# Grouped softmax on one core: tiles of 24 groups in four buffers, in place of 16 groups in six

## The chip, the core and the metric

The kernel runs on one core of a Trainium2 chip. A core has a matrix engine (PE), VectorE (DVE in the profile), ScalarE (ACT), GpSimd (POOL) and SyncE (SP), which run their own instruction streams and meet at semaphores. Data moves between the chip's main memory (DRAM here, HBM in the profile) and the on-chip memory of 128 partitions (SBUF) by 16 DMA engines, which all queues share. The metric is the device time of one execution in microseconds; the median of four runs is compared.

## The reference

The input is 4 x 4096 rows of 4352 floats. Each row falls into 8 groups of 544, and each group gets its own softmax:

```python
def reference(x):
    B, N, D = x.shape          # 4, 4096, 4352
    G = 8
    Dg = D // G                # 544
    x_g = x.reshape(B, N, G, Dg)
    x_g = x_g - x_g.max(axis=-1, keepdims=True)
    exp = np.exp(x_g)
    out = exp / exp.sum(axis=-1, keepdims=True)
    return out.reshape(B, N, D).astype(np.float32)
```

285.2 MB are read and 285.2 MB written. A group is 544 x 4 = 2176 bytes, and there are 131,072 groups, 1024 for each of the 128 partitions.

## The kernel before

The 16,384 rows are cut into 64 tiles of 256 rows. A tile puts two consecutive rows on each partition, 16 groups or 34,816 bytes that lie side by side in DRAM (L33, L34). Six buffers `xt` of that size take the tiles in turn (tile t in buffer t mod 6, L51); exp, sums and products are done in place.

For each tile the work goes round the engines:

- SP issues the load (L126) after the store of the tile six before from the same buffer has landed (L123). The last tile is loaded in two halves (L129).
- ScalarE takes exp of the whole tile in one instruction (L75), as soon as the load has landed.
- VectorE sums the groups into `sums`, which lies in PSUM (L85), takes reciprocals of the 16 sums into `rs` (L87), and multiplies the tile by them, each broadcast over its group (L90).
- POOL waits for that product and issues the store (L138). The stores of the last two tiles are issued by SP instead (L134).

So loads go through SP's queue (q1 in the profile) and stores through POOL's (q0), and within each queue the order is that of the tiles. The instruction streams of all engines are written out tile by tile, with no loop.

No maximum is subtracted on this way. Instead all sums are kept in PSUM until the end, and `judge` (L97 to L119) tests whether one lies outside 1e-6 to 1e30: the largest and the smallest of the sums by two reductions each (L101, L103), two comparisons (L106, L109), a product with ones on PE that counts over the partitions (L113), a sum and a cast (L117, L119). Only where the count isn't zero is everything computed again, with the maximum subtracted (from L156). With this input that branch isn't taken.

Of the kernel before, what the change touches and what calls it, by code (L numbers as in the profile page):

```python
# [9 lines left out]
def kernel(  # L10
# [6 lines left out]
    G = 8  # L17
    P = 128
    R = 2
    NT = 6  # L20
    RG = R * G
# [4 lines left out]
    nt = N // (P * R)  # L26
    LAST = 2
    LOW, HIGH = 1e-6, 1e30
    f32 = mybir.dt.float32
    X = mybir.AxisListType.X  # L30
    Exp = mybir.ActivationFunctionType.Exp
    op = mybir.AluOpType
    xt = xf.rearrange("(t p r) d -> t p (r d)", p=P, r=R)  # L33
    ot = of.rearrange("(t p r) d -> t p (r d)", p=P, r=R)  # L34

    landed = [tc.alloc_semaphore(f"landed{b}") for b in range(NT)]
    stored = [tc.alloc_semaphore(f"stored{b}") for b in range(NT)]
    last_landed = tc.alloc_semaphore("last_landed")
# [4 lines left out]
    scaled = tc.alloc_semaphore("scaled")  # L43
    tested = tc.alloc_semaphore("tested")
# [6 lines left out]
    bufs = [ctx.enter_context(nc.sbuf_tensor(f"xt{b}", [P, R * D], f32)) for b in range(NT)]  # L51
    rs = ctx.enter_context(nc.sbuf_tensor("rs", [P, NT, RG], f32))
    mx = ctx.enter_context(nc.sbuf_tensor("mx", [P, RG], f32))
    sm = ctx.enter_context(nc.sbuf_tensor("sm", [P, RG], f32))
    one = ctx.enter_context(nc.sbuf_tensor("one", [P, 1], f32))
    extreme = ctx.enter_context(nc.sbuf_tensor("extreme", [P, 4], f32))
    outside = ctx.enter_context(nc.sbuf_tensor("outside", [P, 4], f32))
    count = ctx.enter_context(nc.sbuf_tensor("count", [1, 1], f32))
    verdict = ctx.enter_context(nc.sbuf_tensor("verdict", [1, 1], mybir.dt.int32))
    half = nt // 2  # L60
    sums = [ctx.enter_context(nc.psum_tensor(f"sums{h}", [P, half, RG], f32)) for h in range(2)]
    found = ctx.enter_context(nc.psum_tensor("found", [1, 4], f32))

    parts = [(t, slice(0, RG)) for t in range(nt - 1)]
    parts += [(nt - 1, slice(r * G, (r + 1) * G)) for r in range(R)]

    def grouped(b):
        return bufs[b][:, :].rearrange("p (g d) -> p g d", d=Dg)

    def groups(t, g):  # L70
        return grouped(t % NT)[:, g, :]

    def scalar_exp(n):
        t, g = parts[n]
        i = nc.scalar.activation(out=groups(t, g), in_=groups(t, g), func=Exp, scale=1.0)  # L75
        if g.start == 0:
            i.wait_op(landed[t % NT], 16 * (t // NT + 1), "sem-ge")
        else:
            i.wait_op(last_landed, 16, "sem-ge")
        i.then_inc(exp_done, 1)  # L80

    def vector_scale(n):
        t, g = parts[n]
        s = sums[t // half][:, t % half, g]
        nc.vector.reduce_sum(out=s, in_=groups(t, g), axis=X).wait_op(  # L85
            exp_done, n + 1, "sem-ge").then_inc(sum_done, 1)
        nc.vector.reciprocal(out=rs[:, t % NT, g], in_=s).wait_op(  # L87
            sum_done, n + 1, "sem-ge").then_inc(rec_done, 1)
        xg = groups(t, g)
        nc.vector.tensor_tensor(  # L90
            out=xg,
            in0=xg,
            in1=rs[:, t % NT, g].unsqueeze(2).to_broadcast([P, g.stop - g.start, Dg]),
            op=op.mult,
        ).wait_op(rec_done, n + 1, "sem-ge").then_inc(scaled, 1)

    def judge():  # L97
        nc.vector.memset(one[:, :], 1.0).then_inc(tested, 1)  # L98
        flat = [s[:, :, :].rearrange("p t g -> p (t g)") for s in sums]
        for h in range(2):  # L100
            nc.vector.tensor_reduce(  # L101
                out=extreme[:, h:h + 1], in_=flat[h], axis=X, op=op.max).then_inc(tested, 1)
            nc.vector.tensor_reduce(  # L103
                out=extreme[:, 2 + h:3 + h], in_=flat[h], axis=X, op=op.min).then_inc(tested, 1)
        nc.vector.wait_ge(tested, 5)
        nc.vector.tensor_scalar(  # L106
            out=outside[:, 0:2], in0=extreme[:, 0:2], scalar1=HIGH, scalar2=None,
            op0=op.is_gt).then_inc(tested, 1)
        nc.vector.tensor_scalar(  # L109
            out=outside[:, 2:4], in0=extreme[:, 2:4], scalar1=LOW, scalar2=None,  # L110
            op0=op.is_lt).then_inc(tested, 1)
        nc.tensor.wait_ge(tested, 7)
        nc.tensor.matmul(  # L113
            out=found[:, :], lhsT=one[:, :], rhs=outside[:, :],
            start=True, stop=True).then_inc(counted, 1)
        nc.vector.wait_ge(counted, 1)
        nc.vector.reduce_sum(out=count[:, :], in_=found[:, :], axis=X).then_inc(tested, 1)  # L117
        nc.vector.wait_ge(tested, 8)
        nc.vector.tensor_copy(out=verdict[:, :], in_=count[:, :]).then_inc(judged, 1)  # L119

    for t in range(nt):
        if t >= NT:
            nc.sync.wait_ge(stored[t % NT], 16 * (t // NT))  # L123
        tile_in = bufs[t % NT]
        if t < nt - 1:
            nc.sync.dma_start(out=tile_in[:, :], in_=xt[t]).then_inc(landed[t % NT], 16)  # L126
        else:
            for r in range(R):
                nc.sync.dma_start(  # L129
                    out=tile_in[:, r * D:(r + 1) * D], in_=xt[t, :, r * D:(r + 1) * D],  # L130
                ).then_inc(landed[t % NT] if r < R - 1 else last_landed, 16)
# [13 lines left out]
    for n in range(len(parts)):  # L145
        scalar_exp(n)
# [74 lines left out]
```

## Time and profile before

| What | Value |
|---|---|
| median of four runs | 1325.15 us (1325.03 to 1325.25) |
| the profiled execution, its own time | 1325.08 us |
| its span in the trace | 1323.3 us |
| VectorE busy | 1199.3 us, 91% |
| ScalarE busy | 478.7 us, 36% |
| POOL busy | 33.3 us, 3% |
| read and written | 285.21 MB each, 431 GB/s over the span |
| load, median from issue to landing | 41.4 us |
| POOL's store, median from issue to landing | 55.4 us |
| ScalarE's wait for loads, in total | 815.3 us |
| SP's wait (L126) for stores, in total | 1196.1 us |

The span is the time from the first to the last instruction of the program in the trace; the run's own time has a little more around it. In the rows that follow, a timeline line is start, duration, engine, line of the kernel, operation, what it writes and reads, and in brackets how long the engine had been idle and what ended that. A group line has the number of instructions, then their busy time in all and the mean of one in ns, then the idle time before them. A window line has from:to and length, busy time of PE, PEld, DVE, ACT and POOL (with the number of instructions), PE's clock, the share of the DMA engines that was busy, and GB/s. A DMA queue's row has packets, MB, and the share of the 16 engines' time that its packets took.

### The profile page before, as it was taken

The numbers are of one execution on the slowest core, as the hardware profiler recorded it, in microseconds if no ns is written. First come the engines' busy times: TensorE is split into PE (matmuls) and PEld (weight loads), VectorE is DVE, ScalarE is ACT, GpSimd is POOL, SyncE is SP. The second block draws the span as 40 slices with busy tenths as digits, with TensorE's granted clock in tenths as the row PEclk, the third lists the DMA queues.
The fourth block names the chain that finished last, engine by engine and source line by source line (L and its number), as shares of the span: only waits on it lengthen the run. The fifth ranks groups of instructions, "written<-read, shape, count | busy, mean of one in ns | idle before, by whom it ended". The sixth has DMA issues, their size and how long they took to land.

```text
span 1323.3 us, 475 instructions
## 1 busy us (share of the span) xinstructions
PE 0.2 (0%) x2; PEld 0.1 (0%) x2; DVE 1199.3 (91%) x204; ACT 478.7 (36%) x66; POOL 33.3 (3%) x66
## 2 busy tenths in 40 slices
PE   0000000000000000000000000000000000000000
PEld 0000000000000000000000000000000000000000
DVE  3999999999898988989989889898898988989895
ACT  4443342433424324234243342433424334243231
POOL 0000000000000000000000000000000000000000
DMA  9999999999999999999999999999999999999999
GB/s 404 421 437 429 430 438 435 430 431 437 434 429 435 436 434 429 436 436 433 428 437 437 430 430 437 434 431 433 436 434 430 435 436 433 429 436 437 430 429 389
DMA packets 18581, 570.47 MB, mean 431 GB/s; under 512 B 2064, under 2 KB 2064, under 8 KB 2064
## 3 DMA queue, kind: packets, MB, share of 16 engines
q1 hardware_dynamic: 9648, 294.13, 51.6%
q0 software_dynamic: 8928, 276.30, 48.3%
q14 instruction: 5, 0.04, 0.0%
HBM read 285.21 MB, written 285.21 MB: 431 GB/s over the span
## 4 chain that ended last, share of the span: by engine, by line
another core or an unknown queue 67%; DVE 21%; DMA 8%; ACT 1%; SPq 1%; issue 0%; PE 0%; POOLq 0%
DVE xt L90 10%; DVE sums L85 10%; DMA xt<-in_x_dram 4%; DMA out_dram<-xt 4%; ACT xt L75 1%; SPq L126 1%; DVE rs L87 0%; DVE extreme L103 0%; DVE extreme L101 0%; PE found L113 0%; DVE outside L106 0%; DVE count L117 0%; DVE verdict L119 0%; DVE outside L109 0%
## 5 line engine op out<-in xcount | busy, mean ns | idle before, releaser
L75 ACT ACTIVATE xt<-xt 128x8704 f32<-128x8704 f32 (+1 forms) x65 | 477.4, 7345 | 815.3 <-DMA xt<-in_x_dram 815.3
L85 DVE TENSOR_REDUCE sums<-xt 128x16 f32<-128x8704 f32 (+1 forms) x65 | 590.6, 9086 | 104.7 <-ACT xt L75 104.7
L90 DVE TENSOR_TENSOR xt<-xt,rs 128x8704 f32<-128x8704 f32 (+1 forms) x65 | 590.5, 9085 | 2.3
L138 POOL DMA_DIRECT2D out_dram<-xt x62 | 33.1, 533 | 1233.2 <-DVE xt L90 1233.2
L87 DVE RECIPROCAL rs<-sums 128x16 f32<-128x16 f32 (+1 forms) x65 | 16.6, 256 | 2.2
L144 ACT ACT_TABLE_LOAD x1 | 1.3, 1283 | 0.9 <-PEq L205 0.9
L101 DVE TENSOR_REDUCE extreme<-sums 128x1 f32<-128x512 f32 x2 | 1.4, 684 | 0.0
L103 DVE TENSOR_REDUCE extreme<-sums 128x1 f32<-128x512 f32 x2 | 1.4, 682 | 0.0
L117 DVE TENSOR_REDUCE count<-found 1x1 f32<-1x4 f32 x1 | 0.1, 149 | 0.3 <-PE found L113 0.3
L113 PE MATMUL found<-outside,one 128*1 128x4 f32 x2 | 0.2, 166 | 1308.3 <-DVE outside L109 1308.3
L106 DVE TENSOR_SCALAR outside<-extreme 128x2 f32<-128x2 f32 x1 | 0.2, 170 | 0.0
L119 DVE CAST verdict<-count 1x1 int32<-1x1 f32 x1 | 0.1, 141 | 0.0
L113 PEld LDWEIGHTS found<-outside,one 128*1 128x1 f32 x2 | 0.1, 80 | 1308.3 <-DVE outside L109 1308.3
L109 DVE TENSOR_SCALAR outside<-extreme 128x2 f32<-128x2 f32 x1 | 0.2, 163 | 0.0
L205 POOL MEMSET const-float32-0.0<- 128x1 f32 x1 | 0.1, 99 | 0.3 <-issue 0.3
L205 POOL MEMSET const-bfloat16-1.0<- 128x1 bf16 x1 | 0.1, 102 | 0.0
L205 POOL MEMSET const-float32-1.0<- 128x1 f32 x1 | 0.1, 99 | 0.0
L205 POOL MEMSET const-uint8-127<- 128x1 uint8 x1 | 0.1, 99 | 0.0
L98 DVE MEMSET one<- 128x1 f32 x1 | 0.1, 59 | 0.0
## 6 DMA issues: line engine op xcount, KB each, us to landing
xt<-in_x_dram SPq DMA_DIRECT2D x63, 4352.0 KB, 41.4
out_dram<-xt POOLq DMA_DIRECT2D x62, 4352.0 KB, 55.4
out_dram<-xt SPq DMA_DIRECT2D x2, 4352.0 KB, 20.6
xt<-in_x_dram SPq DMA_DIRECT2D x2, 2176.0 KB, 43.3
```

Source lines behind the costliest of these rows:

```text
L75: i = nc.scalar.activation(out=groups(t, g), in_=groups(t, g), func=Exp, scale=1.0)
L85: nc.vector.reduce_sum(out=s, in_=groups(t, g), axis=X).wait_op(exp_done, n + 1, "sem-ge").then_inc(sum_done, 1)
L87: nc.vector.reciprocal(out=rs[:, t % NT, g], in_=s).wait_op(sum_done, n + 1, "sem-ge").then_inc(rec_done, 1)
L90: nc.vector.tensor_tensor(out=xg, in0=xg, in1=rs[:, t % NT, g].unsqueeze(2).to_broadcast([P, g.stop - g.start, Dg]), op=op.mult,).wait_op( ...
L101: nc.vector.tensor_reduce(out=extreme[:, h:h + 1], in_=flat[h], axis=X, op=op.max).then_inc(tested, 1)
L103: nc.vector.tensor_reduce(out=extreme[:, 2 + h:3 + h], in_=flat[h], axis=X, op=op.min).then_inc(tested, 1)
L106: nc.vector.tensor_scalar(out=outside[:, 0:2], in0=extreme[:, 0:2], scalar1=HIGH, scalar2=None, op0=op.is_gt).then_inc(tested, 1)
L113: nc.tensor.matmul(out=found[:, :], lhsT=one[:, :], rhs=outside[:, :], start=True, stop=True).then_inc(counted, 1)
L126: nc.sync.dma_start(out=tile_in[:, :], in_=xt[t]).then_inc(landed[t % NT], 16)
L138: nc.gpsimd.dma_start(out=ot[t], in_=bufs[t % NT][:, :]).then_inc(stored[t % NT], 16)
L144: nc.scalar.preload_act_table(Exp)
L205: nc = _bacc.Bacc("TRN2", target_bir_lowering=False, num_devices=1)
```

## The change

Tiles are cut by groups instead of rows. A partition of an ordinary tile takes 24 groups, 52,224 bytes side by side in DRAM, in four buffers of that size. The first tile has 16 groups, then come 41 of 24, then one of 16 and one of 8: 44 tiles. The last tile is no longer loaded in halves; SP still issues the stores of the last two tiles and POOL the others.

ScalarE takes exp in parts of at most 12 groups, and VectorE sums each part when its exp is done; reciprocal and product stay one instruction per tile. The sums lie in SBUF now (`vals`), beside the reciprocals, and after each product one more instruction keeps the largest sum and the largest reciprocal of each place in `peak`. At the end `judge` reduces `peak` alone.

ScalarE's and VectorE's streams are no longer written out: tile 0 stands by itself, then a loop of ten turns has four tiles to a turn (one for each buffer), then tiles 41 to 43. So that the waits in the loop can be on constants, the engine that waited counts its semaphores down again: ScalarE `landed` after each tile, VectorE four semaphores at the end of each turn. SP and POOL stay written out. The branch that computes again is adapted to the new buffers.

```diff
-    R = 2
-    NT = 6
-    RG = R * G
+    NT = 4
+    LAST = 2
+    C = 12
...
+    per = N * G // P
+    T = 3 * G
+    sizes = [16] + [T] * (per // T - 1) + [16, 8]
+    nt = len(sizes)
+    turns = (nt - 1 - LAST) // NT
+    start = [sum(sizes[:t]) for t in range(nt + 1)]
+    xg_all = xf.rearrange("n (g d) -> (n g) d", d=Dg)
+    og_all = of.rearrange("n (g d) -> (n g) d", d=Dg)
...
+    def dram(a, t):
+        lo, hi = start[t] * P, start[t + 1] * P
+        return a[lo:hi, :].rearrange("(p g) d -> p (g d)", p=P)
+
+    def parts(t):
+        return [(c, min(c + C, sizes[t])) for c in range(0, sizes[t], C)]
...
+    bufs = [ctx.enter_context(nc.sbuf_tensor(f"xt{b}", [P, T * Dg], f32)) for b in range(NT)]
+    vals = ctx.enter_context(nc.sbuf_tensor("vals", [P, NT, 2, T], f32))
+    peak = ctx.enter_context(nc.sbuf_tensor("peak", [P, 2, T], f32))
...
+    def scalar_tile(t, landed_at):
+        b = t % NT
+        for k, (lo, hi) in enumerate(parts(t)):
+            i = nc.scalar.activation(
+                out=groups(b, lo, hi), in_=groups(b, lo, hi), func=Exp, scale=1.0)
+            if k == 0:
+                i.wait_op(landed[b], landed_at, "sem-ge")
+            i.then_inc(exp_done, 1)
+
+    def vector_tile(t, exp_at, at):
+        b = t % NT
+        size = sizes[t]
+        for k, (lo, hi) in enumerate(parts(t)):
+            i = nc.vector.reduce_sum(
+                out=vals[:, b, 0, lo:hi], in_=groups(b, lo, hi), axis=X).wait_op(
+                exp_done, exp_at + k + 1, "sem-ge")
+        i.then_inc(sum_done, 1)
+        nc.vector.reciprocal(out=vals[:, b, 1, :size], in_=vals[:, b, 0, :size]).wait_op(
+            sum_done, at + 1, "sem-ge").then_inc(rec_done, 1)
+        xg = groups(b, 0, size)
+        nc.vector.tensor_tensor(
+            out=xg, in0=xg,
+            in1=vals[:, b, 1, :size].unsqueeze(2).to_broadcast([P, size, Dg]),
+            op=op.mult,
+        ).wait_op(rec_done, at + 1, "sem-ge").then_inc(scaled, 1)
+        nc.vector.tensor_tensor(
+            out=peak[:, :, :size], in0=peak[:, :, :size], in1=vals[:, b, :, :size], op=op.max,
+        ).wait_op(kept, at + 1, "sem-ge").then_inc(kept, 1)
...
     for t in range(nt):
         if t >= NT:
             nc.sync.wait_ge(stored[t % NT], 16 * (t // NT))
...
+        nc.sync.dma_start(out=buf(t), in_=dram(xg_all, t)).then_inc(landed[t % NT], 16)
     for t in range(nt - LAST, nt):
+        nc.sync.wait_ge(scaled, t + 1)
+        nc.sync.dma_start(out=dram(og_all, t), in_=buf(t)).then_inc(last_stored, 16)
 
     for t in range(nt - LAST):
         nc.gpsimd.wait_ge(scaled, t + 1)
+        nc.gpsimd.dma_start(out=dram(og_all, t), in_=buf(t)).then_inc(stored[t % NT], 16)
...
     nc.scalar.preload_act_table(Exp)
-    for n in range(len(parts)):
-        scalar_exp(n)
-
-    for n in range(len(parts)):
-        vector_scale(n)
-    judge()
+    scalar_tile(0, 16)
+    nc.scalar.sem_inc(landed[0], -16)
+    with nc.scalar.Fori(0, turns):
+        for t in looped:
+            scalar_tile(t, 16)
+            nc.scalar.sem_inc(landed[t % NT], -16)
+    for t in rest:
+        scalar_tile(t, 16)
+
+    nc.vector.memset(peak[:, :, :], 0.0).then_inc(kept, 1)
+    vector_tile(0, 0, 0)
+    for s, n in ((exp_done, before[1]), (sum_done, 1), (rec_done, 1), (kept, 1)):
+        nc.vector.sem_inc(s, -n)
+    with nc.vector.Fori(0, turns):
+        for k, t in enumerate(looped):
+            vector_tile(t, before[t] - before[1], k)
+        for s, n in ((exp_done, turn), (sum_done, NT), (rec_done, NT), (kept, NT)):
+            nc.vector.sem_inc(s, -n)
+    for k, t in enumerate(rest):
+        vector_tile(t, before[t] - before[rest[0]], k)
+    judge(len(rest))
```

## The prediction

> **What bounds the kernel now.** I read the page first: the DMA row and the queues.
>
> ```profile
> span 1323.3 us, 475 instructions
> ...
> DMA  9999999999999999999999999999999999999999
> ...
> q1 hardware_dynamic: 9648, 294.13, 51.6%
> q0 software_dynamic: 8928, 276.30, 48.3%
> q14 instruction: 5, 0.04, 0.0%
> ```
>
> The 16 DMA engines are full in all 40 slices, and the packets of the two queues took 99.9% of the span between them. Is that one limit or two (read and write)? I asked the windows view for a stretch with loads alone, one with both, and the end. The last two columns are the DMA share and GB/s.
>
> ```profile
> 10.00:40.00 30.00, 0.00 (x0) 0.00 (x0) 18.62 (x3) 20.48 (x3) 0.00 (x0) 1.00 1.00 432
> 300.00:1200.00 900.00, 0.00 (x0) 0.00 (x0) 820.68 (x133) 322.79 (x45) 23.37 (x44) 1.00 1.00 433
> 1240.00:1320.00 80.00, 0.19 (x2) 0.09 (x2) 64.68 (x22) 22.19 (x4) 1.06 (x2) 1.00 1.00 432
> ```
>
> Loads alone and loads with stores run at the same rate, so the engines themselves are the limit, from the first load to 1320 us. VectorE is second: 820.68 of 900 us. For the fixed cost of a transfer I need two sizes, and the end of ScalarE's timeline has them: the last tile's load is in two halves, and each start below is a landing.
>
> ```profile
> 1260.18 7.46 ACT L75 ACTIVATE xt<-xt 128x8704 f32<-128x8704 f32 x1 [13.11 <-DMA xt<-in_x_dram]
> 1275.63 3.83 ACT L75 ACTIVATE xt<-xt 128x4352 f32<-128x4352 f32 x1 [7.99 <-DMA xt<-in_x_dram]
> 1291.07 3.83 ACT L75 ACTIVATE xt<-xt 128x4352 f32<-128x4352 f32 x1 [11.61 <-DMA xt<-in_x_dram]
> ```
>
> A load and a store of 16 groups (8.913 MB) take 20.573 us: (1260.18 - 66.94) / 58, where 66.94 is the start for tile 4 (shown with the start of the kernel below). A half load and a whole store (6.685 MB) take 15.445 us. The difference, 2.228 MB in 5.128 us, is 434.5 GB/s; 8.913 MB at that rate are 20.51 us, and 0.06 is left for two transfers. The trace's packet records say it more finely: 34,816 bytes took 1288 ns and 17,408 took 648 ns on one engine, so 640 ns for 17,408 bytes, which is 27.2 bytes/ns (435.2 GB/s on 16) and 8 ns besides. By this rate 20.573 leaves 0.093, and 15.445 leaves 0.085: about 0.045 us for each transfer, whatever its size. The bytes alone need 570.43 MB / 435.2 GB/s = 1310.7 us, and all that any tiling can win lies in the other 12.6 us of the span.
>
> **The change, part by part.**
>
> *Fewer, longer transfers.* There were 65 loads and 64 stores; there are 44 and 44, of the same bytes. 41 fewer at 0.045 us is -1.85. The ends: 0.03 (the first estimate above) gives -1.2; the packet records unoverlapped, eight times 8 ns and a closing one of 9 ns, give 0.073 and -3.0. I take -1.85, because two sizes agree on it.
>
> The Trainium skill (DMA: Bandwidth & Descriptors, Anatomy of one DMA) puts about 2.0 us of fixed cost on each DMA. As a cost of throughput that would make this part -82 us; the 0.045 us of the trace says that a full queue hides it.
>
> *Instruction fetches.* The page's q14 row shows five packets of 8 KB inside the span. One of them takes one DMA engine for about 0.3 us (8 KB at 27.2 bytes/ns), and a transfer lands when its slowest engine is done. Unrolled code for 64 tiles becomes loops on ScalarE and VectorE and 44 DMA issues on POOL and SP. From 0 (as many as before, or others that the loops cause) to -0.8 (three fewer on the slowest engine); I take -0.4.
>
> *VectorE per tile.* Rows by form:
>
> ```profile
> L85 DVE TENSOR_REDUCE sums<-xt 128x16 f32<-128x8704 f32 x63 | 581.2, 9226 | 104.7 <-ACT xt L75 104.7
> L90 DVE TENSOR_TENSOR xt<-xt,rs 128x8704 f32<-128x8704 f32 x63 | 581.1, 9224 | 2.2
> L75 ACT ACTIVATE xt<-xt 128x8704 f32<-128x8704 f32 x63 | 469.8, 7457 | 795.7 <-DMA xt<-in_x_dram 795.7
> L87 DVE RECIPROCAL rs<-sums 128x16 f32<-128x16 f32 x63 | 16.2, 258 | 2.2
> L90 DVE TENSOR_TENSOR xt<-xt,rs 128x4352 f32<-128x4352 f32 x2 | 9.4, 4692 | 0.1
> L85 DVE TENSOR_REDUCE sums<-xt 128x8 f32<-128x4352 f32 x2 | 9.4, 4686 | 0.0
> ```
>
> Sizes 16 and 8 give 0.5675 us a group and 0.146 fixed for the reduction, so 12 groups are 6.96; 0.5665 and 0.16 for the product, so 24 are 13.76. A tile of 24 is 2 x 6.96 + 0.31 (reciprocal) + 13.76 + the new maximum into peak. That has no row: from 0.17 (the 2-element compare of the check) to 0.68 (its 512-element reduction); 0.25, nearer the small one. Sum 28.2 us. The DMA needs 13.37 MB / 435.2 + 0.09 = 30.8 us for that tile's load and store, so VectorE has 2.6 us to spare per tile, 10.3 per turn of four: nothing on the path. Beside the DMA lie also ScalarE (two parts of 0.2 + 12 x 0.454 = 5.6 us in 30.8) and the shorter final check.
>
> *The loops.* No row shows a turn: ten back edges, four decrements on VectorE, four on ScalarE. From about 0.2 us (a few instructions like the 33 ns compare-and-branch at the end of POOL) to 5.6 us, the longest delay of a cold transfer here: the first store landed 26.2 us after its issue, 5.6 over the 20.57 that its packets take among a load's. Queued behind a late back edge are VectorE's next reduction, then the store that POOL issues. Even 5.6 is under the 10.3 spare. I take 0.5 a turn, hidden; without that cover it would be 5 us.
>
> The skill speaks against this part (Runtime: NRT & Kernel Launch, Instruction fetch mechanics): a taken branch out of the two-page window waits for a fetch. No row here shows such a wait; if every turn had one, the sum would still be what the 5.6 us end gives.
>
> *Four buffers.* A buffer's round is 4 x 30.8 = 123 us, as 6 x 20.57 was. About 34 us of it is compute (5.6 + 28.2), 26 before, so load and store keep 89 us for 31 us of their own packets: both queues stay backed up. SP's wait for stores (1196 us in all) changes nothing as long as the engines have the other queue's packets.
>
> *The start*, the one place where both queues can run dry:
>
> ```profile
> 13.82 7.46 ACT L75 ACTIVATE xt<-xt 128x8704 f32<-128x8704 f32 x1 [11.63 <-DMA xt<-in_x_dram]
> 21.31 9.23 DVE L85 TENSOR_REDUCE sums<-xt 128x16 f32<-128x8704 f32 x1 [21.31 <-ACT xt L75]
> 30.87 9.22 DVE L90 TENSOR_TENSOR xt<-xt,rs 128x8704 f32<-128x8704 f32 x1
> 40.40 0.67 POOL L138 DMA_DIRECT2D out_dram<-xt  x1 [39.95 <-DVE xt L90]
> ...
> 66.94 7.46 ACT L75 ACTIVATE xt<-xt 128x8704 f32<-128x8704 f32 x1 [13.11 <-DMA xt<-in_x_dram]
> ```
>
> Now exp is in parts of 12 and 4: VectorE starts at 13.8 + 5.7 = 19.5 and scales tile 0 by 38.4 (6.96 + 2.42 + 0.3 + 9.22). Four loads and store 0 are 104 groups, 66.9 us of DMA at 10.29 per 16, so they end near 69.5 (start 1.9, first packets slow by 0.7). Next come load 4, which must wait for store 0, and store 1, scaled at 38.4 + 28.2 = 66.6. Store 0 shares the engines with a load of longer packets: 8 x (1.28 + 1.92) = 25.7 us and up to 5.6 of delay from 38.7 make it 64 to 70; load 4 moves some 1.4 us after that (landing to wait 0.4, issue to first packet 1.0), store 1 some 4 us after 66.6. The gap is between 0 and 2 us; the earlier of the two fills it, so I take 0.3. In the old kernel six loads were queued and this could not happen.
>
> *The end.* Before, tile 63's last half landed at 1291.07 and was scaled 14.5 us later (1305.6), while stores kept the DMA busy to about 1321.4, 30.3 us after that landing; the last store needs 10.3 of them and 1.4 to get moving, so 4 us of cover were left. Now load 42 alternates with packets of 24 groups (8 x (1.28 + 1.92) = 25.7 us after load 41) and load 43 too (8 x (0.64 + 1.92) = 20.5). VectorE scales tile 43 at 33.8 + 19.2 + 9.8 = 62.8 us after the landing of tile 41, 16.6 after that of tile 43. With the same 30 us of stores left, 30 - 16.6 - 5.2 - 1.4 = 7 us of cover: I cost it at 0. Without cover each microsecond that VectorE is late would count in full.
>
> Sum on the profiled execution: 1323.3 - 1.85 - 0.4 + 0.3 = 1321.35 us span. That execution took 1325.08 us and the median is 1325.15, so 1.85 us lie around the span: **1323.2 us**.
>
> **The rivals.**
> - *VectorE becomes the bound through its loop.* At ten back edges, from 10.3 us a turn on; beyond that ten times the excess: 15 us a turn is +47, 1370 us. For it: VectorE is 91% busy. Against: 10.3 us is nearly twice the longest delay seen. Chance 0.08, slower.
> - *The start runs dry twice* (near 70 and 100 us, when load 5 and store 2 come late as well), because loop entry holds VectorE up to 5.6 us. +2 to +4 in place of 0.3: 1325 to 1327, seldom more. For it: the times above meet within 2 us. Against: both would have to be late. Chance 0.18.
> - *The rows are cut.* If 52,224 bytes go as two packets, the change doesn't make transfers cheaper: 88 x 17 - 129 x 9 = 335 more packets per engine at 5 ns (0.045 / 9) is +1.7; with fetches and gap 1326.7. Against: 34,816 went as one. Chance 0.06.
>
> **How the numbers follow.** The forecast has 0.68, its own range 1322.0 to 1324.6. 0.2% (2.65 us, about what a measurement of this kernel can tell from no change) puts the border at 1322.5, which the forecast reaches if fetches give their -0.8 or a transfer costs nearer 0.073: 0.27 of its 0.68. Slower is the first rival, 0.04 of the second and 0.03 for what I don't see: 0.15. The rest, 0.58, is within 0.2%. The range 1322.0 to 1326.7 takes in the start and the cut rows and leaves out the loop.
>
> **What would show it.** Landings of whole tiles 30.8 us apart in the middle; 12,672 packets in q1 and q0 together; GB/s over the span up by 0.6; DMA idle at 69 to 71 us or not; reductions at the loop's head waiting for ScalarE, not for nothing. It is wrong if VectorE is never idle in the middle, or if the spacing exceeds 31 us.

## The result, and the profile after

| | before | after |
|---|---|---|
| own time, median | 1325.11 us (68 runs) | 1326.41 us (42 runs) |
| lowest to highest | 1324.75 to 1325.55 | 1324.05 to 1337.85 |
| span, median of the executions | 1323.4 us | 1323.7 us |
| own time less span, median | 1.76 us | 2.54 us |
| the profiled execution, span and own time | 1323.3, 1325.08 us | 1322.8, 1325.08 us |

The ratio is 1.0019, with a 95% interval of 1.0013 to 1.0025 (this ratio and those below weigh all the times; the ratio of the two medians is 1.0010): the changed kernel is a little slower, where 0.15% faster was forecast. More telling than the median is the width. The kernel before repeats within 0.8 us; the changed one reaches 13.8 us above its own lowest time, and its lowest is 1.06 us under the old median.

The page of the profiled execution after, with its DMA row and queues:

```profile
span 1322.8 us, 604 instructions
...
DMA  9999999999999999999999999999999999999998
...
q1 hardware_dynamic: 6624, 291.90, 51.1%
q0 software_dynamic: 6048, 278.53, 48.6%
q14 instruction: 2, 0.02, 0.0%
```

12,672 packets in q1 and q0, as forecast: rows of 52,224 bytes are not cut. Instruction packets fell from five to two. Only the last slice is no longer full. The windows view (columns as before) puts numbers to it:

```profile
300.00:1200.00 900.00, 0.00 (x0) 0.00 (x0) 816.78 (x147) 325.84 (x59) 15.40 (x29) 1.00 1.00 434
1240.00:1300.00 60.00, 0.00 (x0) 0.00 (x0) 57.13 (x13) 22.56 (x5) 1.06 (x2) 1.00 1.00 432
1300.00:1320.00 20.00, 0.19 (x2) 0.09 (x2) 10.04 (x10) 0.00 (x0) 0.00 (x0) 1.00 0.91 393
```

The last of these lines for the kernel before:

```profile
1300.00:1320.00 20.00, 0.19 (x2) 0.09 (x2) 8.46 (x12) 0.00 (x0) 0.00 (x0) 1.00 0.97 420
```

In the middle the engines are full at 434 GB/s (433 before). From 1300 to 1320 us the share is 0.91, where it was 0.97. By the packet records no engine is idle in either kernel from 60 to 1318 us; in after nine of the 16 have closed their last transfer by 1318.83 us, and the other seven go on. Landings, by ScalarE's starts in the timeline, two in the middle and the last three:

```profile
599.12 11.18 ACT L92 ACTIVATE xt<-xt 128x6528 f32<-128x6528 f32 x2 [19.69 <-DMA xt<-in_x_dram]
629.98 11.18 ACT L92 ACTIVATE xt<-xt 128x6528 f32<-128x6528 f32 x2 [19.69 <-DMA xt<-in_x_dram]
...
1247.18 11.18 ACT L92 ACTIVATE xt<-xt 128x6528 f32<-128x6528 f32 x2 [19.62 <-DMA xt<-in_x_dram]
...
1272.88 7.55 ACT L92 ACTIVATE xt<-xt 128x6528 f32<-128x6528 f32 x2 [14.52 <-DMA xt<-in_x_dram]
...
1294.12 3.83 ACT L92 ACTIVATE xt<-xt 128x4352 f32<-128x4352 f32 x1 [13.69 <-DMA xt<-in_x_dram]
```

The spacing is (1247.18 - 599.12) / 21 = 30.86 us for a load and a store of 24 groups; 30.8 (30.81 with one more digit) was forecast. A difference of 0.05 looks like nothing, but a load lands when its last engine is done, so it is the last engine's pace, and there are 41 such tiles. The rows of VectorE and ScalarE by form:

```profile
L102 DVE TENSOR_REDUCE vals<-xt 128x12 f32<-128x6528 f32 x84 | 580.2, 6947 | 111.0 <-ACT xt L92 111.0
L109 DVE TENSOR_TENSOR xt<-xt,vals 128x13056 f32<-128x13056 f32 x41 | 564.1, 13758 | 1.4
L92 ACT ACTIVATE xt<-xt 128x6528 f32<-128x6528 f32 x84 | 469.5, 5635 | 804.9 <-DMA xt<-in_x_dram 804.9
L106 DVE RECIPROCAL vals<-vals 128x24 f32<-128x24 f32 x41 | 12.4, 303 | 1.4
L114 DVE TENSOR_TENSOR peak<-peak,vals 128x48 f32<-128x48 f32 x41 | 8.3, 201 | 0.0
```

2 x 6.95 + 0.30 + 13.76 + 0.20 = 28.2 us a tile, the forecast to the digit, and VectorE's 111.0 us of idle time are all waits for ScalarE. So the rates of the forecast came true, and the time did not. What the rows don't show lies one level down, in the trace's packet records. A transfer has eight rows for each of the 16 DMA engines and ends with one closing packet for each; its semaphore is complete when the last of these 16 is in. The records don't name the engine, but the times tell it: a packet begins 3 to 4 ns before the one ahead of it on its engine ends. From the records I took three numbers for each kernel's profiled execution: how many packets after 60 us lasted over 30 ns longer than 8 ns + bytes / 27.2 (long packets); the largest spread between the first and the last of the 16 closing packets of one transfer between 200 and 1200 us (the lag); and the time by which a load is issued before the first engine is done with the load ahead of it (the reserve, median of the same stretch; below zero, the load comes too late for that engine). The times are of all executions.

```
                 buffers  row, bytes     long     lag, us       reserve  own time, us
                 x groups                packets  load  store   us       lowest .. median .. highest (runs)
before           6 x 16   34,816            8      1.6    2.8    19.1    1324.75  1325.11  1325.55 (68)
after            4 x 24   52,224           49      2.5    3.8     2.7    1324.05  1326.41  1337.85 (42)
e1_unrolled      4 x 24   52,224          193      6.8   20.0     1.7    1325.41  1329.02  1336.24 (10)
e2_loops16       6 x 16   34,816           11      1.6    2.2    19.4    1324.69  1325.33  1326.16 (11)
e3_part24        4 x 24   52,224          170      7.7   15.4     2.6    1329.00  1337.76  1343.84 (7)
e4_part6         4 x 24   52,224          163      8.0   23.4     1.5    1325.54  1337.28  1339.11 (12)
e5_t16_four      4 x 16   34,816           48      2.0    2.0     3.6    1335.81  1336.22  1336.99 (5)
e6_t20_four      4 x 20   43,520          215      9.8   19.4    -1.4    1336.23  1336.84  1338.31 (5)
e7_t19_five      5 x 19   41,344           22      5.2    2.2    13.0    1325.37  1326.58  1327.57 (11)
f1_first24       4 x 24   52,224          123      2.4    4.2     2.9    1329.80  1330.90  1339.27 (6)
f2_first8_six    6 x 16   34,816           69      6.4    3.2    29.3    1325.28  1326.04  1329.29 (11)
f3_t12_eight     8 x 12   26,112            6      2.0    2.8    41.3    1327.75  1328.35  1328.61 (9)
f4_first19       5 x 19   41,344           27      4.0    4.0     6.4    1325.55  1327.70  1330.31 (11)
g1_load_halves   4 x 24   26,112/52,224  1846     25.3    5.0     3.9    1381.87  1388.63  1390.79 (5)
g4_halves        4 x 24   26,112            4      2.2    2.2     4.3    1326.63  1327.53  1327.74 (11)
g5_halves_early  4 x 24   26,112            4      2.3    1.9     5.2    1329.79  1330.86  1331.35 (5)
k1_gap           4 x 24   26,112           37      2.9    2.3     6.4    1326.18  1326.84  1328.66 (11)
k2_nogap         4 x 24   52,224           56      2.9    4.0     2.6    1324.49  1325.76  1334.31 (12)
h1_first8        4 x 24   52,224          184     11.9   23.9    -2.6    1335.96  1338.43  1339.03 (4)
```

(In the g kernels the reserve is that of a tile's first half.) In the profiled execution of after the median engine closed its last transfer at 1318.82 us (before: 1320.32), the last engine at 1320.88 (before: 1321.46). The typical engine gained 1.50 us of the forecast 1.95 (1.85 + 0.4 - 0.3); the one that sets the end gained 0.58, and this was one of the good executions. In it the engines fall into two groups: the nine with at most 0.4 us of long packets after 60 us closed at 1318.3 to 1318.8 us, the seven with 1.1 to 1.9 us at 1320.0 to 1320.9.

### The profile page after: what moved, and what is told of

Read it like the earlier page. It is cut to its first block, busy times and chain, and to the rows that moved or that the text cites. A ratio compares the mean times of both kernels' runs of the same rounds, so it can differ in the third digit from the quotient of the medians.

```text
span 1322.8 us, 604 instructions
## 1 busy us (share of the span) xinstructions
PE 0.2 (0%) x2; PEld 0.1 (0%) x2; DVE 1195.0 (90%) x226; ACT 478.4 (36%) x88; POOL 22.6 (2%) x46
## 4 chain that ended last, share of the span: by engine, by line
another core or an unknown queue 71%; DVE 17%; DMA 7%; issue 2%; ACT 1%; SPq 1%; DVEq 0%; PE 0%; POOLq 0%
DVE vals L102 9%; DVE xt L109 7%; DMA xt<-in_x_dram 4%; DMA out_dram<-xt 4%; ACT xt L92 1%; SPq L139 1%; DVE vals L106 0%; DVE peak L114 0%; DVE within L124 0%; DVE extreme L120 0%; PE found L128 0%; DVEq L170 0%; DVE count L132 0%; DVE verdict L134 0%
## 5 line engine op out<-in xcount | busy, mean ns | idle before, releaser
L92 ACT ACTIVATE xt<-xt 128x6528 f32<-128x6528 f32 (+1 forms) x87 | 477.2, 5531 | 818.6 <-DMA xt<-in_x_dram 818.6
L102 DVE TENSOR_REDUCE vals<-xt 128x12 f32<-128x6528 f32 (+1 forms) x87 | 589.5, 6817 | 111.0 <-ACT xt L92 111.0
L109 DVE TENSOR_TENSOR xt<-xt,vals 128x13056 f32<-128x13056 f32 (+2 forms) x44 | 587.2, 13346 | 1.5
L146 POOL DMA_DIRECT2D out_dram<-xt x42 | 22.4, 534 | 1258.7 <-DVE xt L109 1258.7
L106 DVE RECIPROCAL vals<-vals 128x24 f32<-128x24 f32 (+2 forms) x44 | 13.1, 298 | 1.5
L114 DVE TENSOR_TENSOR peak<-peak,vals 128x48 f32<-128x48 f32 (+2 forms) x44 | 8.8, 200 | 0.0
## 6 DMA issues: line engine op xcount, KB each, us to landing
out_dram<-xt POOLq DMA_DIRECT2D x41, 6528.0 KB, 52.9
out_dram<-xt POOLq DMA_DIRECT2D x1, 4352.0 KB, 30.8
```

What stands on the lines that cost most here:

```text
L92: i = nc.scalar.activation(out=groups(b, lo, hi), in_=groups(b, lo, hi), func=Exp, scale=1.0)
L102: i = nc.vector.reduce_sum(out=vals[:, b, 0, lo:hi], in_=groups(b, lo, hi), axis=X).wait_op(exp_done, exp_at + k + 1, "sem-ge")
L106: nc.vector.reciprocal(out=vals[:, b, 1, :size], in_=vals[:, b, 0, :size]).wait_op(sum_done, at + 1, "sem-ge").then_inc(rec_done, 1)
L109: nc.vector.tensor_tensor(out=xg, in0=xg, in1=vals[:, b, 1, :size].unsqueeze(2).to_broadcast([P, size, Dg]), op=op.mult,).wait_op(rec_done ...
L114: nc.vector.tensor_tensor(out=peak[:, :, :size], in0=peak[:, :, :size], in1=vals[:, b, :, :size], op=op.max,).wait_op(kept, at + 1, "sem-g ...
L146: nc.gpsimd.dma_start(out=dram(og_all, t), in_=buf(t)).then_inc(stored[t % NT], 16)
```

## The experiments

All kernels are the changed one with the edit shown, except e8, which is the kernel before.

### Is it the loops, or the time at which VectorE is done?

The first theory was that loops delay VectorE now and then; the rival, that four large buffers do it. e1 writes both loops out; e2 keeps the loops and goes back to six buffers of 16.

```diff
-    with nc.scalar.Fori(0, turns):
+    for _ in range(turns):
...
-    with nc.vector.Fori(0, turns):
+    for _ in range(turns):
```

```diff
-    NT = 4
+    NT = 6
-    C = 12
+    C = 16
-    T = 3 * G
-    sizes = [16] + [T] * (per // T - 1) + [16, 8]
+    T = 2 * G
+    sizes = [T] * (per // T)
```

> The changed kernel with both loops written out, the same instructions otherwise. Theory L (the loops' branches and decrements hold VectorE or ScalarE up, by an amount that differs between executions): the spread of 1324 to 1338 us goes, median near 1323.3, the sum of the prediction. Theory B (four buffers leave too little work queued, so that anything late leaves DMA engines without packets): spread and median stay as they are, near 1326.4 and up to 1335 or more.

> Loops alone: the changed kernel with 64 tiles of 16 groups in six buffers, exp in one part, ten turns of six tiles. Theory L: a spread of several us appears, median above 1326. Theory B: as steady as the kernel before, 1324.3 to 1325.3, with up to 0.8 us gained by fewer instruction fetches.

e1: ratio 1.0034 (1.0017 to 1.0051), executions from 1325.41 to 1336.24. e2: 1.0002 (0.9993 to 1.001), within 1.5 us. Without loops the spread remains, with loops and the old tiles it is gone: the loop theory fell. In the profiled execution after, VectorE's wait ahead of a tile is 2.6 to 3.3 us from the tenth tile to the forty-second, at a loop's head as elsewhere. The Trainium skill (Runtime: NRT & Kernel Launch, Instruction fetch mechanics) would have a taken branch wait for a fetch where its target is out of the window; in these loops no such wait shows (whether a loop's head was ever out of the window, no run here shows).

e3 and e4 change the parts in which ScalarE and VectorE work: one of 24 groups or four of 6. By exp's 5.64 us for 12 groups, the chain from landing to store gets about 5.6 us longer in e3 and 2.8 shorter in e4.

```diff
-    C = 12
+    C = 24          # e3; in e4: C = 6
```

> The changed kernel with exp of a tile of 24 in one part: the first reduction starts 5.4 us later after a landing, nothing else. Theory B: each buffer is held 5.4 us longer, loads are issued later, spread and median grow, by 2 to 10 us. Theory L: no change in the spread, median within 1 us of 1326.4.

> The changed kernel with exp and sums in parts of 6 groups: the first reduction starts 2.7 us earlier after a landing, VectorE pays some 0.3 us a tile for two more reductions. Theory B: buffers come free about 2.4 us earlier, spread and median shrink, median 1324 to 1325.5. Theory L: no change.

e3: 1.0092 (1.006 to 1.0124). e4: 1.0073 (1.0053 to 1.0094), 9 of 12 executions at 1336.9 or above. Both are worse than after, so the shorter chain of e4 did not help: a miss for both theories. But e4's profile shows what a bad execution looks like. Its windows and its last landings:

```profile
1240.00:1300.00 60.00, 0.00 (x0) 0.00 (x0) 56.26 (x15) 19.60 (x8) 1.06 (x2) 1.00 0.95 409
1300.00:1320.00 20.00, 0.00 (x0) 0.00 (x0) 19.86 (x8) 3.92 (x2) 0.00 (x0) 1.00 0.85 366
```

```profile
1286.69 7.64 ACT L92 ACTIVATE xt<-xt 128x3264 f32<-128x3264 f32 x3 [14.31 <-DMA xt<-in_x_dram]
...
1307.25 3.92 ACT L92 ACTIVATE xt<-xt 128x3264 f32<-128x3264 f32 x2 [12.92 <-DMA xt<-in_x_dram]
```

Up to 1200 us this execution moves 434 GB/s like the good one. Then engines run empty (0.95, 0.85) while the last load isn't in: it lands at 1307.25, 13.1 us later than in after (1294.12), and the span is 12.8 us longer (1335.6 against 1322.8). By the packet records one single engine had 15.7 us of long packets (13.8 in loads, 1.8 in stores), the others 1.7 to 6.1. Every load waits for that engine, VectorE's last products wait for the load, and the other 15 engines, which are done early, wait for the last stores. e1's profiled execution is the same with 12.7 us on one engine.

### Buffers, sizes, the first tile

The next seven change NT and the sizes. The lines that take their place in each:

```diff
-    NT = 4
-    sizes = [16] + [T] * (per // T - 1) + [16, 8]
+    NT = 4; T = 16; C = 8;  sizes = [T] * 64                       # e5
+    NT = 4; T = 20; C = 10; sizes = [16] + [T] * 49 + [16, 12]     # e6
+    NT = 5; T = 19; C = 12; sizes = [16] + [T] * 52 + [12, 8]      # e7
+    NT = 4; T = 24; C = 12; sizes = [T] * 42 + [16]                # f1
+    NT = 6; T = 16; C = 16; sizes = [8] + [T] * 63 + [8]           # f2
+    NT = 8; T = 12; C = 12; sizes = [T] * 85 + [4]                 # f3
+    NT = 5; T = 19; C = 12; sizes = [T] * 53 + [9, 8]              # f4
```

> The changed kernel with 64 tiles of 16 groups, but four buffers, exp in halves. Theory Q (four buffers keep too few transfers queued, so the 16 DMA engines get out of step and one of them falls behind): packets longer than 1288 ns in the middle, the landing of a store spread over 4 us or more between first and last engine, times spread over 3 us or more, median above 1326. Theory S (rows of 52,224 bytes are what is slow): as steady as six buffers of 16, 1324.7 to 1326.2, landings spread over 2 us throughout.

> The changed kernel with tiles of 20 groups in four buffers (rows of 43,520 bytes; 52 tiles, the last of 16 and 12). Theory Q: the same depth of about 2.9 tiles in the queues, so the same picture as the changed kernel, some engine 5 us or more behind, median 1326 to 1335. Theory S: another row size, packets at their nominal 1608 ns, median 1324 to 1325.

> The changed kernel with tiles of 19 groups in five buffers (rows of 41,344 bytes; 55 tiles, the last of 12 and 8). Theory Q: 3.9 tiles in the queues in place of 2.9 (4.7 before), the engines stay in step, spread under 1.5 us, median 1324 to 1325 (19 transfers fewer than before are 0.9 us). Theory S: says nothing of this row, at most as slow as the changed kernel.

Against before: e5 1.0085 (1.0071 to 1.0099), e6 1.0089 (1.0075 to 1.0103), e7 1.001 (1.0001 to 1.0019). e5 is the one to read closely. It has four buffers, yet its engines stay in step (lag 2.0), and its five times lie within 1.2 us. What it loses, it loses at the two ends, where its engines have nothing to do; between 60 and 1300 us the records show none of them idle:

```profile
40.00:60.00 20.00, 0.00 (x0) 0.00 (x0) 19.93 (x7) 9.49 (x3) 0.53 (x1) 1.00 0.98 390
...
1300.00:1320.00 20.00, 0.00 (x0) 0.00 (x0) 18.67 (x5) 4.94 (x2) 0.00 (x0) 1.00 0.63 273
```

Its last load lands at 1297.39 us, that of e2, with six such buffers, at 1280.69; from there exp, sums and product of 16 groups take 22.7 us in e5 and 26.2 in e2 (where tile 62 is still ahead), and from 1300 to 1320 us e5's DMA share is 0.63 (0.97 in e2). By the records its engines are idle for 1.4 us between 40 and 60 us and for some 8 us from 1310 us on. That is a different fault from the one of e4, although both have about 1336 us. e7 is a miss: with 13 us of reserve it was expected in step, within 1.5 us and at 1324 to 1325; it has 1326.58, a width of 2.2 us and a lag of 5.2.

> The changed kernel with a first tile of 24 and one last tile of 16. Theory M (a first tile of another size puts the 16 DMA engines out of step, because loads and stores that alternate have different lengths; an engine out of step then has slow load packets): no packets over nominal in the middle, executions within 1 us of each other; the end costs some us more, since tile 42 of 16 is the last (as with 16 groups in four buffers), 1326 to 1333. Theory S (row sizes other than 34,816 bytes have slow packets by themselves): slow packets all the way, one engine 5 to 15 us behind, executions spread over 3 us or more.

> Tiles of 16 groups in six buffers with the changed kernel's loops, but a first and a last tile of 8. Theory M: some engine gets out of step at the start and loses 3 us or more on load packets in the middle; executions spread. Theory S and theory Q (too few transfers queued): as steady as with 64 equal tiles, no slow packets in the middle, 1324.7 to 1326.

> 86 tiles of 12 groups (rows of 26,112 bytes) in eight buffers, first tile like the others. Theory S: slow packets in the middle although the queues are deep, some engine 3 us or more behind. Theories M and Q: none; then 172 transfers in place of 129 at 0.045 us make 1.9 us more than before, 1326.5 to 1327.5, executions within 1 us of each other.

> Tiles of 19 groups in five buffers, first tile of 19 too (last of 9 and 8). Theory M: the engine that lost 3.3 us on load packets is gone, 1324 to 1325. Theory S: it stays, 1326 to 1327.

f1 1.006 (1.0041 to 1.0079), f2 1.0008 (0.9999 to 1.0017), f3 1.0024 (1.0014 to 1.0034), f4 1.0018 (1.0009 to 1.0027). f3 has tiles of 12 and is steady, so it isn't every size but 16; f4 has a first tile of the common size and still spreads over 4.8 us, so it isn't the odd first tile, though in f2, with six buffers and a reserve of 29 us, a first tile of 8 alone brought long packets all through the first 235 us of the execution. So each of the theories Q, S and M misses at least one of the seven kernels. In f1 the first store comes 14.6 us later than in after (53.36 against 38.72); the engines idle for 1.2 us between 80 and 100 us, and long packets take 2.8 us of each engine. The rest of its loss I can't place. Down the table the lag grows with the row: 2 to 3 us at 26,112 and 34,816 bytes (6.4 in f2), 4 to 5 at 41,344, 4 to 24 from 43,520 on. But longer rows also mean fewer buffers.

e8 asked whether the long packets that the kernel before has at 42 to 45 us, some 2 us after its first store is issued (31 packets, about 1 us on each engine; the table's 8 come later), come from POOL's queue. ScalarE issues each store after exp of the next tile:

```diff
-        nc.gpsimd.wait_ge(scaled, t + 1)
-        nc.gpsimd.dma_start(out=ot[t], in_=bufs[t % NT][:, :]).then_inc(stored[t % NT], 16)
+        nc.scalar.wait_ge(scaled, t + 1)
+        nc.scalar.dma_start(out=ot[t], in_=bufs[t % NT][:, :]).then_inc(stored[t % NT], 16)
```

> The kernel before with its stores issued by ScalarE's queue (each after the exp of the next tile) in place of POOL's. Measures the 0.5 to 0.8 us by which all engines' load packets are stretched, twice, around 42 to 45 us, where POOL issues the first store. If that is POOL's way of issuing, some 1 us is gained: 1324.1. If any first store does it, no change.

1.0004 (0.9995 to 1.0013), with 30 such packets at the first store, at 41 to 45 us. They belong to the first store, whoever issues it: in f1, where it is issued at 53.36 us, they come at 54 to 58, in f2 (23.30) at 24 to 30.

### Length of the packets, or reserve of the load queue?

The reserve fell from 19.1 us to 2.7, which made "the load queue is too shallow" the best theory; packets too long was its rival. g4 halves every load and store of a 24-group tile, with the same buffers and order; g5 also takes exp of the first half as soon as it is in; g1 halves the loads alone.

```diff
-        nc.sync.dma_start(out=buf(t), in_=dram(xg_all, t)).then_inc(landed[t % NT], 16)
+        for lo, hi in pieces(t):        # (0, 12), (12, 24)
+            nc.sync.dma_start(out=bufp(t, lo, hi), in_=dramp(xg_all, t, lo, hi)).then_inc(landed[t % NT], 16)
```

> The changed kernel with every load and every store of a 24-group tile issued as two transfers of 12 groups (26,112 bytes per partition) back to back; still four buffers of 24 groups, ScalarE still waits until the whole tile has landed. 170 transfers in place of 88. Theory 'packet length' (packets of 52,224 bytes are what goes wrong): no over-long load packets in the middle, executions within about 1.5 us of each other, median about 1327 (1325.1 plus 41 more transfers than the kernel before at 0.045 us). Theory 'shallow load queue' (with four buffers the next load is issued too late): nothing changes for the engine that falls behind; executions spread over 5 us or more, some at 1330 and above, and landings of one store spread by 5 us or more among the DMA engines late in the execution.

> As the kernel with halves, and ScalarE takes exp of a tile's first half as soon as that half has landed, so that the chain from a load's landing to its store gets about 6 to 10 us shorter. Theory 'shallow load queue': the next load is issued about 6 to 10 us earlier relative to the landing before it, the spread goes down to 1.5 us or less, median about 1327. Theory 'packet length': the same as the kernel with halves alone. If both theories are wrong, the spread stays at 5 us or more in both kernels.

> The changed kernel with only the loads of 24-group tiles in two transfers of 12 groups; stores stay whole. 129 transfers, as many as in the kernel before. Theory 'packet length' of the loads: no over-long load packets, executions within 1.5 us, median about 1325.1 (the kernel before's). Theory 'packet length' of the stores (a load packet waits behind a long store packet): the spread remains here and is gone where both are halved. Theory 'shallow load queue': the spread remains here, 1326 to 1338.

g4: 1.0016 (1.0007 to 1.0025), all 11 executions within 1.11 us, lag 2.2, median 0.5 us over the expected 1327. That is what the theory of the packets' length expected, and not what the other did, in a kernel whose buffers and tiles are those of after. g5 is in step too, at 1.0043 (1.0029 to 1.0057), 3.9 us above its expectation. In its profiled execution, 2.1 us longer than g4's, the excess lies behind the last packet: 4.4 us pass from there to the end of the span, in g4 1.9. Why is open.

g1 was a miss of all theories: 1.0472 (1.0449 to 1.0496), 63 us. From the page's DMA issues (transfers, KB each, median us from issue to landing), the lines of g1, then those of g4:

```profile
xt<-in_x_dram SPq DMA_DIRECT2D x82, 3264.0 KB, 48.8
out_dram<-xt POOLq DMA_DIRECT2D x41, 6528.0 KB, 30.0
```

```profile
xt<-in_x_dram SPq DMA_DIRECT2D x82, 3264.0 KB, 34.6
out_dram<-xt POOLq DMA_DIRECT2D x82, 3264.0 KB, 37.8
```

While both queues have work, an engine takes a packet of one and a packet of the other in turn, so a queue with packets half as long gets half the bytes: in the records of the kernel before, 99% of successive packets on an engine between 300 and 1200 us are of different queues. The Trainium skill (DMA: Bandwidth & Descriptors, Queues, rings and completion order) says that an engine goes round its queues packet by packet; these rows agree. g1's stores overtake, its store queue runs empty in every tile (a store is issued some 5.6 us after the first engine is done with the one ahead), and each new store is followed by a burst of long load packets on nearly all engines: of 789 load packets that were over 100 ns too long, 688 ended 2 to 6 us after a store's issue. Long packets make up 45 us per engine, most of the loss: 27 in loads and 18 in stores. What lengthens the stores' packets, the burst doesn't explain.

One rival was left: that twice as many transfers wait in g4. k1 keeps the 88 transfers and puts a gap of 64 bytes between the halves of each buffer, so that a row goes as two packets; k2 is the same kernel without the gap.

```diff
+    GAP = 16
+    H = C * Dg + GAP
-    bufs = [ctx.enter_context(nc.sbuf_tensor(f"xt{b}", [P, T * Dg], f32)) for b in range(NT)]
+    bufs = [ctx.enter_context(nc.sbuf_tensor(f"xt{b}", [P, 2 * H], f32)) for b in range(NT)]
...
+    def halves(t):
+        return bufs[t % NT][:, :].rearrange("p (h x) -> p h x", h=2)[:, :, :C * Dg]
```

> The changed kernel, 88 transfers, same order and same four buffers, but each 24-group buffer has a gap of 64 bytes between its two halves of 12 groups, so that a row of a tile must go as two packets of 26,112 bytes (23,168 packets in q1 and q0 together in place of 12,672). VectorE's product runs over both halves in one instruction. Theory 'packet length': no engine falls behind, executions within about 1.5 us, median about 1326.8 (the kernel with loads and stores in halves had 1327.5 with 82 more closing packets per engine, worth 0.7). Theory 'transfers queued' (what helped the halves was that twice as many transfers were waiting): an engine falls behind again, landings of one store spread by 5 us or more late in the execution, executions from 1326 to 1340.

> The same kernel as the one with the gap, with the gap set to 0: the same instructions, packets of 52,224 bytes again if the two halves are joined (12,672 packets). Control for the gap. Theory 'packet length': an engine falls behind in some executions as in the changed kernel, median 1326 to 1330, executions over a range of 5 us or more. Theory 'transfers queued': no difference between this kernel and the one with the gap but for the packets' own cost of about 1.7 to 3 us.

(In k2 GAP is 0.) The queues on k1's page, and then on k2's:

```profile
q1 hardware_dynamic: 11872, 291.90, 51.2%
q0 software_dynamic: 11296, 278.53, 48.8%
```

```profile
q1 hardware_dynamic: 6624, 291.90, 51.1%
q0 software_dynamic: 6048, 278.53, 48.6%
```

k1: 1326.84, ratio 1.0016 (1.0007 to 1.0024), highest 2.5 us over the lowest. k2: 1325.76, 1.002 (1.0006 to 1.0033), highest 9.8 us over the lowest. k1's median is the expected one, its width 2.5 us where 1.5 was expected; k2's median is 0.2 under the expected range. In after 20 of 42 executions lie more than 2.5 us above its lowest (the border is k1's own width, chosen with the result known), so eleven that don't would come by chance once in some 1200 times ((22/42) to the 11th). Against k2 alone, where four of twelve do, it is weaker: chance would put all four there once in some 18 times. With the transfers the same, and g4 beside it, short packets keep the executions together. They cost what they save: k1's spans begin at 1323.9 us, k2's at 1322.2, and its median is 1.1 us longer.

The table has a catch, though. The short packets also raised the reserve, from 1.5 to 2.9 us in the kernels with rows of 52,224 bytes to 4.3 to 6.4 us. The last run was to part the two, with long packets and a larger reserve, by shifting loads against stores:

```diff
-    sizes = [16] + [T] * (per // T - 1) + [16, 8]
+    sizes = [8] + [T] * (per // T - 1) + [16, 8, 8]
```

> The changed kernel with a first tile of 8 groups in place of 16 and last tiles of 16, 8 and 8 (45 tiles): packets of 52,224 bytes and four buffers as before, but the streams of loads and stores are shifted against each other. In the kernels with 19 groups in five buffers a first tile smaller by 3 groups raised the reserve (the time by which the next load is issued before the first engine is done with the load ahead of it) from 6.4 to 13.0 us, taken from the reserve of the stores (31.9 to 24.4); here 8 groups should raise it from 1.6 to 2.7 us to 8 us or more, of the 21 us that loads and stores have together. Theory 'reserve': the load queue no longer comes close to running out, engines stay in step (lag of 3 us or less), executions within 2.5 us, median 1324 to 1325. Theory 'packet length by itself': long load packets and a lag of 4 us or more remain, executions over 5 us or more, median 1325 to 1330. If the reserve doesn't rise above 4 us, nothing is told apart.

1.0095 (1.0078 to 1.0112). The reserve went the wrong way, to -2.6, and by its own terms the run tells nothing apart. It adds one point: with e6 it is the second kernel whose reserve is below zero, and these two have lags of 19 and 24 us in their profiled executions and no execution under 1335.9. So whether a row of 52,224 bytes lengthens packets by itself, or by what it leaves of the reserve, stays open; a lag eats reserve too, since a store lands with its last engine and the reserve is measured to the first.

Two readings of the kept records bear on this. The table's reserve is that of the load queue alone. By the same measure the store queue has 32.0 us in the kernel before and 18.2 in after, but -2.8 in e6 and -4.1 in h1 (g1: -5.8), so in these two the stores come too late as well as the loads. And e4 shows an order: between 130 and 260 us its loads still have 5 to 6 us of reserve and its stores 16 to 20, and long packets come all the same; by 890 us the lag of its stores has grown from 2 to 21 us and their reserve has fallen to 2. So there an empty queue isn't what starts the lag, and the lag then eats the reserve. k1 and g4 have no long packets from 300 to 900 us, at 6.4 and 4.3 us of reserve, which speaks for the length of the row; but e3, which has 5.3 us from 130 to 440 us, has next to none there either.

No kernel here beats the one before; e2 can't be told from it.

## Why the prediction was wrong

- **Fewer, longer transfers, -1.85.** This is the step that failed: "about 0.045 us for each transfer, whatever its size". The median packet of 52,224 bytes took 1928 ns, exactly 8 + bytes / 27.2; the spacing was right to 0.05 us, and the typical engine ended 1.5 us earlier. But a price from packets of 17,408 and 34,816 bytes was carried to longer ones and to all 16 engines alike. In after single engines meet long packets (39 of the table's 49 are loads), and the end hangs on the slowest one. I had written that "a transfer lands when its slowest engine is done", and used it for instruction fetches only. The missing term, single engines falling behind, is 0.45 us at best (lowest span 1321.8 against the forecast 1321.35), 2.4 in the median (1323.7) and 14 at worst (1335.4). Of after only a good execution was profiled; that its slow ones are like those of e1 and e4 is inferred. That short packets in the same buffers take the wide part of it away is shown (g4, k1); by which way is not.
- **Four buffers, 0.** "Both queues stay backed up" was true of the profiled execution: no engine idled in the middle. That the reserve ahead of the next load would shrink from 19.1 to 2.7 us I hadn't worked out. Of the 89 us for load and store, the page gives the load 36.0 and the store 52.9 (median to landing); and a load beside a store's packets takes 30.8 us for itself, so the load queue had some 5 us to spare, not 58. What four buffers cost with tiles of 16, so with a third fewer bytes on the chip, is seen in e5: 11 us. What four of 24 cost by themselves no run isolates.
- **Around the span, 1.85.** It is 1.76 in the kernel before and 2.54 after, in the median: 0.7 us more than I allowed. With the 2.4 above it makes up nearly all of the 3.2 between 1323.2 and 1326.41. The nine kernels in which POOL issues 41 to 43 stores have 1.9 to 2.7, those with 50 or more, and e8 with none, 1.7 to 1.8; no run isolates the cause.
- **Instruction fetches, -0.4.** Two packets in place of five, both at 1316 us. Before, the last engine had two of them and closed 0.8 us after the next one (1321.46 against 1320.69), so the size was about right.
- **VectorE per tile, the loops.** Right: 28.2 us, maximum into peak 0.20 (taken as 0.25); no delay at the loop's head. The rival of a VectorE-bound loop is out.
- **The start, 0.3.** Store 1 was issued at 66.68, forecast 66.6; the packet records show no idle time between 60 and 100 us, so the 0.3 was nothing. The rival that runs dry twice is out. So is that of the cut rows. k1, whose gap does cut them, has the median 1326.84 where that rival was given 1326.7; part of this is luck, since its span is 0.7 us shorter than the rival's sum has it (1324.2 against 1324.9) and 0.75 us more lie around it.
- **The end, 0.** The last product ended at 1309.31, 15.2 us after the last landing (forecast 16.6); in the profiled execution stores covered it. Where the last load is late, that cover is gone and each microsecond counts in full: 13.1 late in e4, 12.8 in the span.
- **The signs of being wrong.** Neither came: VectorE waits 2.6 to 3.3 us a tile and the spacing is 30.86 us. Both watch what the forecast had right; none watched the spread between engines or between executions.

## What to carry to other kernels

Where the DMA engines bound a kernel, its end is that of the slowest of the 16; a better mean rate is worth little until the spread of the closing packets has been looked at, and a single profile may show a good execution. Look at the width of the times beside the median: a kernel that repeats within 0.8 us and one that ranges over 14 differ in kind, and the profile to read is the bad one. Where two queues share the engines, keep their packets equally long: halving one side alone cost 63 us here.

## What the runs showed of the hardware

- Single DMA engines fall behind the others by up to 24 us (h1), through packets, of loads above all, that last up to 1.9 us longer than 8 ns + bytes / 27.2 (e3). What makes such a packet long isn't known; in e1 and e4 they come at all distances from the issue of a load or a store.
- A store that starts on an empty store queue lengthens load packets on nearly every engine, 2 to 6 us after its issue: once in the kernel before (by up to 0.8 us a packet, some 1 us an engine), in each tile of g1.
- Where nothing lags, a transfer more costs little and steadily: g4, with 170 in place of 129, took 2.1 us more than before, f3, with 172, 3.2 us. If all of it is put down to the transfers, an estimate, that is 0.05 and 0.07 us each.
